# Interleaving two arrays: the first tile as two sub-tiles that are contiguous in HBM

## The chip, the cores and the metric

The kernel runs on one core of a Trainium2 chip. The metric is the time of one execution on the device in microseconds (us). For the kernel before, the median of three runs is 314.14 us (314.09 to 314.22).

The core has 16 DMA engines that move data between HBM and the on-chip memory (SBUF, 128 partitions). DMAs are issued here from two queues: SyncE's (SP, named q1 in the profile) and ScalarE's (ACT, named q10). VectorE (DVE) does the copying inside SBUF. The engines run at their own pace and wait for each other through semaphores; a DMA adds 16 to its semaphore when all of it has landed.

## The reference

The inputs x and y are float32 arrays of 32 x 256 x 1024 elements (33.6 MB each). The output has twice as many elements in its last dimension, with x in the even and y in the odd places:

```
result = np.zeros((batch, seq, dim * 2), dtype=np.float32)
result[..., 0::2] = x
result[..., 1::2] = y
```

There is no arithmetic. 67.1 MB are read and 67.1 MB are written.

## The kernel before

All three arrays are taken as flat. A tile is 128 partitions by W = 8192 elements of x and of y, 32 KiB a partition (4 MiB of each input), and gives 64 KiB a partition of output. There are n = 8 tiles, k = 0 to 7. H = W/2 = 4096 is half a tile's row. The function `rows` gives tile k of an array as 128 rows that adjoin in HBM, so a whole tile of input has rows of 32 KiB, 32 KiB apart, and a tile of output has rows of 64 KiB.

In SBUF there are two buffers each for x, y and the output (`xt`, `yt`, `ot`). Tile k uses xt and yt number k % 2. Its output is made in two halves, h = 0 and 1, and half h always goes to ot number h.

Three engines have work, each in its own order:

- SP issues the loads (lines 42 to 53). The first tile of x comes in two DMAs: columns 0 to H (line 42, semaphore xsem[0]) and columns H to W (line 43, semaphore hsem), both with rows of 16 KiB that lie 32 KiB apart in HBM. Then come y's first tile in one DMA, and x and y of tile 1, all without a wait. From tile 2 on, x waits for the third of the four copies of tile k - 2 (line 48) and y for the fourth (line 51), through the semaphore `woven`, which counts copies.
- VectorE makes four copies a tile, for each half one of x into the even places of ot (line 67) and one of y into the odd places (line 70). Before half 0 it waits for x's load (line 60) and, ahead of the copy of y, for y's load (line 69). For tile 0, half 1, it waits for hsem (line 62). From tile 1 on, it waits until the store of the preceding tile from the same buffer is complete (line 64), and for tile 1, half 0, also for qsem (line 66).
- ACT issues the stores (lines 72 to 85), each after the two copies that fill the half. A store takes 32 KiB from each partition to HBM rows that lie 64 KiB apart. The very first is cut into a quarter (8 KiB rows, line 77, semaphore qsem) and the rest (24 KiB rows, line 81, semaphore osem[0]).

At the end ACT waits for the last store from ot0 and clears the semaphores as one range of numbers (lines 87 to 90); SP waits for the last store from ot1 (line 91).

Lines 104 to 122 move the first two DMAs of SP, which wait for nothing, from the body of the program into its opening block, ahead of SP's drain. In the kernel before these are the two halves of x's first tile.

Of the kernel before, what the change touches and what calls it, by code (L numbers as in the profile page):

```python
# [3 lines left out]


def _interleave(nc, x, y, out):
    P = 128
    W = 8192
    H = W // 2  # L10

    total = 1
    for s in x.shape:
        total *= s
    n = total // (P * W)
    assert n * P * W == total

    def rows(ap, names, k):
        flat = ap.rearrange("b s d -> (b s d)")
        return flat[k * names : (k + 1) * names].rearrange("(p w) -> p w", p=P)  # L20

    fp32 = mybir.dt.float32
    xt = [nc.alloc_sbuf_tensor(f"xt{b}", [P, W], fp32).ap() for b in (0, 1)]
    yt = [nc.alloc_sbuf_tensor(f"yt{b}", [P, W], fp32).ap() for b in (0, 1)]
    ot = [nc.alloc_sbuf_tensor(f"ot{b}", [P, W], fp32).ap() for b in (0, 1)]

    xsem = [nc.alloc_semaphore(f"xsem{b}") for b in (0, 1)]
    hsem = nc.alloc_semaphore("hsem")
    qsem = nc.alloc_semaphore("qsem")
    ysem = [nc.alloc_semaphore(f"ysem{b}") for b in (0, 1)]  # L30
    woven = nc.alloc_semaphore("woven")
    osem = [nc.alloc_semaphore(f"osem{b}") for b in (0, 1)]


    cuts = [0, W // 4, W]
    parts = [slice(a, b) for a, b in zip(cuts, cuts[1:])]

    xs = [rows(x, P * W, k) for k in range(n)]
    ys = [rows(y, P * W, k) for k in range(n)]
    os_ = [rows(out, 2 * P * W, k) for k in range(n)]  # L40

    nc.sync.dma_start(out=xt[0][:, :H], in_=xs[0][:, :H]).then_inc(xsem[0], 16)
    nc.sync.dma_start(out=xt[0][:, H:], in_=xs[0][:, H:]).then_inc(hsem, 16)

    for k in range(n):
        b = k % 2
        if k >= 2:
            nc.sync.wait_ge(woven, 4 * (k - 2) + 3)
        if k:
            nc.sync.dma_start(out=xt[b], in_=xs[k]).then_inc(xsem[b], 16)  # L50
        if k >= 2:
            nc.sync.wait_ge(woven, 4 * (k - 2) + 4)
        nc.sync.dma_start(out=yt[b], in_=ys[k]).then_inc(ysem[b], 16)

    for k in range(n):
        b = k % 2
        for h in (0, 1):
            c = slice(h * H, (h + 1) * H)
            if h == 0:
                nc.vector.wait_ge(xsem[b], 16 * (k // 2 + 1))  # L60
            elif k == 0:
                nc.vector.wait_ge(hsem, 16)
            if k:
                nc.vector.wait_ge(osem[h], 16 * k)
            if (k, h) == (1, 0):
                nc.vector.wait_ge(qsem, 16)
            nc.vector.tensor_copy(out=ot[h][:, 0::2], in_=xt[b][:, c]).then_inc(woven, 1)  # L67
            if h == 0:
                nc.vector.wait_ge(ysem[b], 16 * (k // 2 + 1))
            nc.vector.tensor_copy(out=ot[h][:, 1::2], in_=yt[b][:, c]).then_inc(woven, 1)  # L70

    for k in range(n):
        for h in (0, 1):
            nc.scalar.wait_ge(woven, 4 * k + 2 * h + 2)
            if (k, h) == (0, 0):
                for c in parts[:-1]:
                    nc.scalar.dma_start(
                        out=os_[k][:, c], in_=ot[h][:, c]
                    ).then_inc(qsem, 16)
                c = parts[-1]  # L80
                nc.scalar.dma_start(out=os_[k][:, c], in_=ot[h][:, c]).then_inc(osem[h], 16)
                continue
            nc.scalar.dma_start(
                out=os_[k][:, h * W : (h + 1) * W], in_=ot[h]
            ).then_inc(osem[h], 16)

    nc.scalar.wait_ge(osem[0], 16 * n)
    used = sorted(s.num for s in [*xsem, hsem, qsem, *ysem, woven, osem[0]])
    assert used == list(range(used[0], used[-1] + 1)), used
    nc.scalar.sem_clear(range(used[0], used[-1] + 1))  # L90
    nc.sync.nop(nofuse=True).wait_op(osem[1], 16 * n, "sem-ge").then_inc(
        osem[1], -16 * n
    )


def kernel(tc, x, y, out):
    nc = tc.nc
    tc.close()
    tc.compile()

    _interleave(nc, x, y, out)

    blocks = nc.main_func.blocks
    for engine in (mybir.EngineType.SP, mybir.EngineType.SP):
        opening = blocks[0].instructions
        at, moved = next(
            (b, i)
            for b in blocks[1:]
            for i in b.instructions
            if i.engine == engine and i.opcode == "DMACopy"  # L110
        )
        assert not (moved.sync_info and moved.sync_info.on_wait)
        body = at.instructions
        body.remove(moved)
        gate = next(
            n
            for n, i in enumerate(opening)
            if i.engine == engine and i.opcode == "Drain"
        )
        opening.insert(gate, moved)  # L120
        at.instructions = body
        blocks[0].instructions = opening


# [1 line left out]
_INS = ['x', 'y']  # L126
_OUTS = [((32, 256, 2048), 'float32')]


# [23 lines left out]
```

## Time and profile before

| What | Value |
|---|---|
| median of three runs | 314.14 us (314.09 to 314.22) |
| profiled execution: span | 312.9 us (the profile gives no other time of this execution) |
| VectorE busy | 72.0 us, 32 copies of 2.29 to 2.30 us |
| VectorE idle before line 67, until a store is complete | 206.5 us, 14 waits, longest 29.0 |
| VectorE idle before line 70, until y has landed | 12.3 us, 1 wait |
| VectorE idle before line 67, until x has landed | 7.3 us, 1 wait |
| DMA, both directions | 134.22 MB, mean 429 GB/s |

The page cuts the span into 40 equal slices. A digit is the busy share of a slice in tenths, so 9 means 90% or more. The line of a DMA queue has its packets, the MB moved, and the time that its packets took as a share of 16 engines' time. A packet here is what one DMA moves for one partition's row, or one of the small ones that count up a semaphore (under 512 B). Where the share of both queues, the stretch and the number of packets are known, the mean time of one packet on its DMA engine follows: share x length of the stretch x 16 / number of packets. In a timeline a line gives start, duration, engine, line of the kernel, operation, and in brackets how long the engine had been idle and what ended that. The duration of a DMA instruction on SPq or ACTq is that of issuing it.

### The profile page before, as it was taken

To read this page: it belongs to the slowest core of one execution; us is meant where nothing else is said; L and a number is where in the kernel's file an instruction comes from. 1 tells how busy PE (TensorE), PEld (TensorE's weight loads), DVE (VectorE), ACT (ScalarE), POOL (GpSimd) and SP (SyncE) were. 2 spreads that over 40 slices of the span, in tenths; PEclk is the share of its full clock that TensorE was granted. 3 is DMA by queue.
4 is the path that set the end of the run, shared out by engine and by line. 5 is a ranking of instruction groups with operands and counts; after the bars stand their busy time and mean duration, and the time that the engine had idled before them with its cause. 6 is when DMAs were issued, how large, how long until landed. Compare 5 with 4: busy or idle time off the path is not lost.

```text
span 312.9 us, 114 instructions
## 1 busy us (share of the span) xinstructions
DVE 72.0 (23%) x32; POOL 0.2 (0%) x4
## 2 busy tenths in 40 slices
DVE  0216000501305023050220503205032050415410
POOL 0000000000000000000000000000000000000000
DMA  8999999999999999999999999999999999999998
GB/s 337 467 402 436 436 402 419 452 457 415 427 444 411 461 402 469 402 469 402 469 402 465 406 440 432 423 448 402 469 402 469 402 469 402 469 402 448 423 423 381
DMA packets 4896, 134.22 MB, mean 429 GB/s; under 512 B 544, under 2 KB 544, under 8 KB 544
## 3 DMA queue, kind: packets, MB, share of 16 engines
q1 hardware_dynamic: 2448, 67.11, 50.1%
q10 hardware_dynamic: 2448, 67.11, 49.7%
HBM read 67.11 MB, written 67.11 MB: 429 GB/s over the span
## 4 chain that ended last, share of the span: by engine, by line
DMA 82%; DVE 12%; issue 0%
DMA out_dram<-ot 76%; DMA yt<-in_y_dram 6%; DVE ot L70 6%; DVE ot L67 6%
## 5 line engine op out<-in xcount | busy, mean ns | idle before, releaser
L67 DVE COPY ot<-xt 128x4096 f32<-128x4096 f32 x16 | 36.7, 2295 | 213.8 <-DMA out_dram<-ot 206.5
L70 DVE COPY ot<-yt 128x4096 f32<-128x4096 f32 x16 | 36.6, 2288 | 12.3 <-DMA yt<-in_y_dram 12.3
L137 POOL MEMSET const-bfloat16-1.0<- 128x1 bf16 x1 | 0.1, 103 | 0.0
L137 POOL MEMSET const-uint8-127<- 128x1 uint8 x1 | 0.1, 102 | 0.0
L137 POOL MEMSET const-float32-0.0<- 128x1 f32 x1 | 0.1, 100 | 0.2 <-issue 0.2
L137 POOL MEMSET const-float32-1.0<- 128x1 f32 x1 | 0.1, 99 | 0.0
## 6 DMA issues: line engine op xcount, KB each, us to landing
out_dram<-ot ACTq DMA_DIRECT2D x15, 4096.0 KB, 34.1
yt<-in_y_dram SPq DMA_DIRECT2D x8, 4096.0 KB, 41.5
xt<-in_x_dram SPq DMA_DIRECT2D x7, 4096.0 KB, 24.3
xt<-in_x_dram SPq DMA_DIRECT2D x2, 2048.0 KB, 9.5
out_dram<-ot ACTq DMA_DIRECT2D x1, 3072.0 KB, 32.8
out_dram<-ot ACTq DMA_DIRECT2D x1, 1024.0 KB, 16.3
```

Of the source, the lines that this page charges most:

```text
L67: nc.vector.tensor_copy(out=ot[h][:, 0::2], in_=xt[b][:, c]).then_inc(woven, 1)
L70: nc.vector.tensor_copy(out=ot[h][:, 1::2], in_=yt[b][:, c]).then_inc(woven, 1)
L137: nc = _bacc.Bacc("TRN2", target_bir_lowering=False, num_devices=1)
```

## The change

The first tile of 4 MiB of each input is no longer 128 rows of 32 KiB but two sub-tiles of 2 MiB, one behind the other in HBM, each with 128 rows of 16 KiB that adjoin (`narrow(x, 1)`, `narrow(y, 1)`). The first tile of output is likewise two sub-tiles of 4 MiB with 128 adjoining rows of 32 KiB (`narrow(out, 2)`). The sub-tiles go to the same places in SBUF as the halves before. The elements that a partition holds are therefore other ones than before, for x, y and the output alike.

x's first tile comes in two DMAs as before, and y's first tile now does too. The two DMAs of x both count on xsem[0], and the two of y on ysem[0]; hsem is gone. For buffer 0 the count that VectorE waits for is 16 higher, so that for tile 0 it waits for 32 on xsem[0] ahead of its first copy, and for 32 on ysem[0] ahead of the second. The quarter and the rest of the first store, and the second store, go to the sub-tiles of the output. All other tiles are as before.

```diff
-    hsem = nc.alloc_semaphore("hsem")
...
-    nc.sync.dma_start(out=xt[0][:, :H], in_=xs[0][:, :H]).then_inc(xsem[0], 16)
-    nc.sync.dma_start(out=xt[0][:, H:], in_=xs[0][:, H:]).then_inc(hsem, 16)
+    def narrow(ap, names):
+        flat = ap.rearrange("b s d -> (b s d)")
+        cut, end = names * P * H, names * P * W
+        return [
+            flat[a:b].rearrange("(p w) -> p w", p=P) for a, b in ((0, cut), (cut, end))
+        ]
+
+    xa, xb = narrow(x, 1)
+    ya, yb = narrow(y, 1)
+    oa, ob = narrow(out, 2)
+
+    nc.sync.dma_start(out=xt[0][:, :H], in_=xa).then_inc(xsem[0], 16)
+    nc.sync.dma_start(out=xt[0][:, H:], in_=xb).then_inc(xsem[0], 16)
+    nc.sync.dma_start(out=yt[0][:, :H], in_=ya).then_inc(ysem[0], 16)
+    nc.sync.dma_start(out=yt[0][:, H:], in_=yb).then_inc(ysem[0], 16)
 
-    for k in range(n):
+    for k in range(1, n):
...
     for k in range(n):
         b = k % 2
+        landed = 16 * (k // 2 + 1) + (16 if b == 0 else 0)
         for h in (0, 1):
             c = slice(h * H, (h + 1) * H)
             if h == 0:
-                nc.vector.wait_ge(xsem[b], 16 * (k // 2 + 1))
-            elif k == 0:
-                nc.vector.wait_ge(hsem, 16)
+                nc.vector.wait_ge(xsem[b], landed)
...
             if h == 0:
-                nc.vector.wait_ge(ysem[b], 16 * (k // 2 + 1))
+                nc.vector.wait_ge(ysem[b], landed)
...
             if (k, h) == (0, 0):
-                for c in parts[:-1]:
...
-                c = parts[-1]
-                nc.scalar.dma_start(out=os_[k][:, c], in_=ot[h][:, c]).then_inc(osem[h], 16)
-                continue
...
+                Q = W // 4
+                nc.scalar.dma_start(out=oa[:, :Q], in_=ot[h][:, :Q]).then_inc(qsem, 16)
+                nc.scalar.dma_start(out=oa[:, Q:], in_=ot[h][:, Q:]).then_inc(osem[h], 16)
+            elif k == 0:
+                nc.scalar.dma_start(out=ob, in_=ot[h]).then_inc(osem[h], 16)
```

More of the change, by code (lines that the diff above doesn't have):

```diff
@@ L32, in _interleave @@
     osem = [nc.alloc_semaphore(f"osem{b}") for b in (0, 1)]
-    cuts = [0, W // 4, W]
-    parts = [slice(a, b) for a, b in zip(cuts, cuts[1:])]
     xs = [rows(x, P * W, k) for k in range(n)]
@@ L48, in _interleave @@
             nc.sync.wait_ge(woven, 4 * (k - 2) + 3)
-        if k:
-            nc.sync.dma_start(out=xt[b], in_=xs[k]).then_inc(xsem[b], 16)
+        nc.sync.dma_start(out=xt[b], in_=xs[k]).then_inc(xsem[b], 16)
         if k >= 2:
@@ L75, in _interleave @@
             if (k, h) == (0, 0):
-                for c in parts[:-1]:
-                    nc.scalar.dma_start(
-                        out=os_[k][:, c], in_=ot[h][:, c]
-                    ).then_inc(qsem, 16)
-                c = parts[-1]
-                nc.scalar.dma_start(out=os_[k][:, c], in_=ot[h][:, c]).then_inc(osem[h], 16)
-                continue
-            nc.scalar.dma_start(
-                out=os_[k][:, h * W : (h + 1) * W], in_=ot[h]
-            ).then_inc(osem[h], 16)
+                Q = W // 4
[3 more added lines that the diff above has]
+                nc.scalar.dma_start(out=ob, in_=ot[h]).then_inc(osem[h], 16)
+            else:
+                nc.scalar.dma_start(
+                    out=os_[k][:, h * W : (h + 1) * W], in_=ot[h]
+                ).then_inc(osem[h], 16)
     nc.scalar.wait_ge(osem[0], 16 * n)
-    used = sorted(s.num for s in [*xsem, hsem, qsem, *ysem, woven, osem[0]])
+    used = sorted(s.num for s in [*xsem, qsem, *ysem, woven, osem[0]])
     assert used == list(range(used[0], used[-1] + 1)), used
```

## The prediction

> **What bounds the kernel now.** I read the page's top first: whether an engine or the transfers fill the span.
>
> ```profile
> span 312.9 us, 114 instructions
> DVE 72.0 (23%) x32; POOL 0.2 (0%) x4
> DMA  8999999999999999999999999999999999999998
> ...
> q1 hardware_dynamic: 2448, 67.11, 50.1%
> q10 hardware_dynamic: 2448, 67.11, 49.7%
> ```
>
> VectorE works 23% of the span; the 16 DMA engines are full in every slice but the first and last, half by loads (q1) and half by stores (q10). The waits say the same: VectorE's 206.5 us before line 67 are waits for stores to free an output buffer. So the end is set by the sum of packet times on a DMA engine, unless a queue runs dry. Next I read packet times, from the DMA view of stretches that start and end between packets.
>
> ```profile
> DMA packets 1152, 33.55 MB, mean 434 GB/s; under 512 B 128, under 2 KB 128, under 8 KB 128
> ...
> q1 hardware_dynamic: 576, 16.78, 50.2%
> q10 hardware_dynamic: 576, 16.78, 50.2%
> ```
>
> This is 100 to 177.4 us, two tiles. Without the 128 small (semaphore) packets there are 1024 of 32 KiB. Their time is 1.004 x 77.4 x 16 = 1243 us, so 1.214 us each. The two queues have equal shares: a store whose rows lie 64 KiB apart in HBM costs what a load of adjoining rows costs.
>
> ```profile
> DMA packets 176, 2.62 MB, mean 430 GB/s; under 512 B 16, under 2 KB 16, under 8 KB 16
> ...
> q1 hardware_dynamic: 176, 2.62, 100.3%
> ```
>
> This is 4 to 10.1 us: 160 packets of 16 KiB, x's first tile. 1.003 x 6.1 x 16 / 160 = 0.612 us each, so two of them cost 0.01 us more than one of 32 KiB. Two stretches were dearer:
>
> ```profile
> DMA packets 64, 1.05 MB, mean 262 GB/s; under 512 B 0, under 2 KB 0, under 8 KB 0
> ...
> q1 hardware_dynamic: 64, 1.05, 76.6%
> ```
>
> 0 to 4 us: 64 packets took 0.766 x 4 x 16 = 49.0 us, 0.766 each, which is (0.766 - 0.612) x 4 = 0.62 us too much per engine: the first packets of the run.
>
> ```profile
> q1 hardware_dynamic: 112, 3.67, 89.7%
> q10 hardware_dynamic: 37, 0.30, 7.1%
> ```
>
> 22 to 32 us, where the first 8 KiB stores join: 112 loads took 0.897 x 160 = 143.5 us, 1.281 each, (1.281 - 1.214) x 7 = 0.47 us too much per engine. Last, the timeline shows what the first tile's arrival releases.
>
> ```profile
> 0.00 0.37 SPq L42 DMA_DIRECT2D xt<-in_x_dram  x1
> ...
> 0.42 0.42 SPq L43 DMA_DIRECT2D xt<-in_x_dram  x1
> 1.90 0.33 SPq L53 DMA_DIRECT2D yt<-in_y_dram  x1
> 2.27 0.43 SPq L50 DMA_DIRECT2D xt<-in_x_dram  x1
> 2.75 0.46 SPq L53 DMA_DIRECT2D yt<-in_y_dram  x1
> 7.33 2.30 DVE L67 COPY ot<-xt 128x4096 f32<-128x4096 f32 x1 [7.33 <-DMA xt<-in_x_dram]
> 21.91 2.29 DVE L70 COPY ot<-yt 128x4096 f32<-128x4096 f32 x1 [12.28 <-DMA yt<-in_y_dram]
> ...
> 24.24 0.38 ACTq L77 DMA_DIRECT2D out_dram<-ot  x1
> ```
>
> The first x copy starts on half of x, then VectorE sits 12.28 us until all of y is there. The second half of x, 11.8 us after its issue by line 43, lands at 0.42 + 11.8 = 12.2. y, third in the queue, lands at 21.9.
>
> **The change part by part.** There is no time of the profiled execution but its span of 312.9; the median of the runs is 314.14, 1.2 more. I take that 1.2 as unchanged and make the sum on the span.
>
> *One wait for both halves of x.* xsem[0] must now reach 32, so the first copy moves from 7.33 to about 12.2 and ends at 12.2 + 2.3 = 14.5. Behind it on VectorE is the wait for y, which ends at 21.9: 7.4 us of slack, cost 0. If y came before 14.5, up to 4.9 us would be on VectorE's path. The later copy of line 67 loses the wait on hsem, which had been over for 12 us: 0.
>
> *y in two DMAs.* The wait is for ysem[0] at 32, both halves, so the first y copy doesn't start on half of y. It stays at the time at which 8 MB have come in. Its packets become 16 per engine of 0.612 instead of 8 of 1.214: 9.79 - 9.71 = +0.08 us, on the path, as the engines are full. One more semaphore packet per engine: the two-tile stretch leaves no more for its 128 than rounding (0.1% of it, 0.08 us per engine, for 8), 0 to 0.01 each; I take 0.01. Below: were 16 KiB as cheap per byte as 32 KiB, 0. Above: at 0.766, the start's price, 16 x (0.766 - 0.607) = +2.5. I take +0.09, because the packets of 4 to 10.1 us are the same size in the same queue without a start.
>
> *SP's queue.* A sixth DMA ahead of SP's first wait. Issues took 0.33 to 0.46 us, so the loads of tile 1 are issued at about 2.7 and 3.2 instead of 2.27 and 2.75. Their first packets run only once y is in, at 21.9: 19 us of cover. Without it the cost would be 0.46. SP's next instruction waits for the third copy, at 26.4. The two DMAs hoisted ahead of the drain are still x's halves, and y's first issue stays at 1.90; ACT's and POOL's queues are passed by nothing.
>
> *Adjoining rows in HBM for x's first halves.* 16 KiB rows are read 16 KiB apart instead of 32. Packets are as many and as large as before, and the trace has no row of exactly this. The nearest are 32 KiB rows that adjoin (1.214) and 16 KiB rows 32 KiB apart (0.612), both at the full rate: 0. Below: the 0.62 of the start could vanish if the start addresses' spacing caused it, -0.62. Above: it could double, +0.62. I take 0, as first packets after nothing is in flight are most simply late for the distance to memory.
>
> *The first output as 32 KiB rows that adjoin.* The quarter's 8 KiB pieces, the 24 KiB rest and the whole second store keep number and size; only their pitch goes from 64 to 32 KiB. In the two-tile stretch pitches of 64 (stores) and 32 (loads) cost the same: 0. The 0.47 where the stores join could vanish or double: -0.47 to +0.47; I take 0, since loads are what ran slow there, and loads there are tile 1's, which the change leaves alone.
>
> *One semaphore fewer.* The clear is one range as before: 0.
>
> Sum: 0 + 0.09 + 0 + 0 + 0 = +0.09, 314.14 + 0.09 = 314.23, call it 314.2. The chain of waits moves by the same 0.1 to its end: stores after the last load run from 278 to 312.5, each buffer's refill (4.5 us of copies) hidden by the other buffer's store of 9.7.
>
> **Rivals.**
>
> *A, faster: the address spacing was the cause of the two dear stretches.* For: they lie at the start and at the first stores, just the transfers that the change moves closer together; everywhere else loads cost 1.214. Against: the steady stretch shows no dependence on pitch, and later 16 KiB packets at the old spacing cost no more than 0.612. Price: both gone, -0.62 - 0.47 + 0.09 = -1.0, 313.1; one of them alone, 313.6 to 313.8. The Trainium skill ("DMA: Bandwidth & Descriptors", Latency and other measured facts) has copies slowed by large power-of-two row pitches and advises laying tiles out contiguously. Its slow cases begin at a 512 KiB pitch, and no pitch here reaches that; the trace's equal shares at 32 and 64 KiB agree that there is nothing to win in the steady part.
>
> *B, slower: an additional DMA pays a start of its own.* The first DMA lands at 7.33, the second, of equal size, 12.2 - 7.33 = 4.9 later: the first paid 2.4 for its start. If y's second half paid that on the engines, 314.2 + 2.4 = 316.6. It decides from 0.63 us of emptiness between two queued DMAs. Against: the second half of x was queued behind the first just so and shows none. The Trainium skill (same page, Anatomy of one DMA) gives about 2.0 us fixed per DMA for DMAs that GpSimd issues. By that the time would be 314.1 + 2.0 = 316.1; the 4.9 us for 2.1 MB, 430 GB/s, disagree for DMAs queued behind another from SP.
>
> *C, slower: reads packed into a narrower part of HBM run slower.* In the first 20 us the 16 engines now read within 2 MB at a time instead of 4. Price from the only row of slowed loads, 1.281 against 1.214, 5.5% of the 19.9 us (2 to 21.9) that the first tile's loads take: +1.1, 315.3. It decides from 3.2% (0.63 of 19.9), 0.63 us per 16 KiB packet. For: no run shows 16 KiB rows adjoining, and HBM is where the change acts. Against: the pitches that are shown cost the same.
>
> *D: the change does nothing for the fill.* It is part of my forecast: neither half of x or y is consumed alone.
>
> **How the numbers follow.** About 0.2%, 0.63 us, is what a measurement of this kernel can tell from no change. Forecast 0.70 at 314.2; its own range is 313.7 (one dear stretch gone) to 314.8 (one doubled). A 0.12, faster by over 0.2%; C 0.14 and B 0.04, slower by over 0.2%. To leave out no more than 2 in 10 I take the half of A and the third of C that lie nearest: 313.4 to 315.0. Faster 0.12, same 0.70, slower 0.18.
>
> **What would show it.** Right: the first line-67 copy starts at 12.2, with a wait for y after it that ends at 21.9 to 22.1; packets of 16 KiB at 0.61 us from 12 to 22; the period of two tiles still 77.4 us; first store issue at 24.3. C is right if y lands after 22.5; B if there is a gap of over 0.6 us in DMA between y's halves; A if 0 to 4 us shows packets near 0.61, or 22 to 32 us loads near 1.214. I'm wrong altogether if a queue runs dry later: a slice of the middle below 9.

## The result and the profile after

The changed kernel takes 314.46 us (median of 19 runs, 314.34 to 316.1), the kernel before 314.21 us beside it (19 runs, 314.08 to 314.6). The medians are 0.25 us apart, 0.08%. The ratio of the two is 1.0016, with a 95% interval of 1.0009 to 1.0022; it lies higher than that of the medians because 7 of the 19 runs of the changed kernel took more than 314.7 us, which none of the kernel before did. The forecast was 314.2, in a range of 313.4 to 315.0, with no change beyond 0.2% as the likeliest: by both figures the time is there, but nearly three times as far above before as the 0.09 of the sum, and with a tail that the forecast didn't have. The interval lies above 1, so here even 0.1% can be told from no change, half of what the prediction took as the least.

The profile of the changed kernel is of the run that took 316.1 us, the longest of the 19. First the top of its page:

```profile
span 314.8 us, 115 instructions
## 1 busy us (share of the span) xinstructions
DVE 72.0 (23%) x32; POOL 0.2 (0%) x4
...
DMA  9999999999999999999999999999999999999996
...
q1 hardware_dynamic: 2592, 67.11, 49.8%
q10 hardware_dynamic: 2448, 67.11, 49.4%
```

The DMA engines are full as before up to the last slice, which has fallen from 8 to 6. q1 has 144 packets more: 128 from y's rows and 16 for the semaphore. Then its timeline of the first tile:

```profile
0.41 0.42 SPq L50 DMA_DIRECT2D xt<-in_x_dram  x1
1.89 0.33 SPq L51 DMA_DIRECT2D yt<-in_y_dram  x1
2.27 0.44 SPq L52 DMA_DIRECT2D yt<-in_y_dram  x1
2.76 0.45 SPq L58 DMA_DIRECT2D xt<-in_x_dram  x1
3.25 0.46 SPq L61 DMA_DIRECT2D yt<-in_y_dram  x1
12.49 2.29 DVE L74 COPY ot<-xt 128x4096 f32<-128x4096 f32 x1 [12.49 <-DMA xt<-in_x_dram]
22.27 2.29 DVE L77 COPY ot<-yt 128x4096 f32<-128x4096 f32 x1 [7.49 <-DMA yt<-in_y_dram]
```

Everything stands in the order forecast, the first copy after both halves of x and a wait of 7.49 us for y behind it, but 0.3 us late: x at 12.49 instead of 12.2, y at 22.27 instead of 22.0. That is past the 22.1 which the prediction named as its last right value for y, and short of rival C's 22.5. Both follow from the start: by the trace's landing events the very first DMA is complete at 7.59 us, in the kernel before at 7.31. The DMA view of 0 to 4 us, and of 14 to 18.9 us, where y is read:

```profile
DMA packets 59, 0.97 MB, mean 242 GB/s; under 512 B 0, under 2 KB 0, under 8 KB 0
...
q1 hardware_dynamic: 59, 0.97, 81.7%
```

```profile
DMA packets 144, 2.10 MB, mean 428 GB/s; under 512 B 16, under 2 KB 16, under 8 KB 16
...
q1 hardware_dynamic: 144, 2.10, 99.9%
```

The first 59 packets took 0.817 x 64 / 59 = 0.886 us each, against 0.766 for the 64 of before. y's packets of 16 KiB took 0.999 x 4.9 x 16 / 128 = 0.612, just as the prediction priced them. The last 7 us (308 to 315), first of the kernel before and then of the changed one:

```profile
DMA  0009900000990000099000000000000000000000
```

```profile
DMA  0499900049990004998000400000040000000000
```

Each digit is 0.175 us, and in so fine a view a packet's time stands in the slice in which it starts. Before, the 16 engines start their packets nearly together. After, 15 of them do so, and one is some 2 us behind: its packets are the single 4s, ahead of the groups of the others and, at the end, alone after the last group. The last store is complete when its slowest engine is. This table has the 16 landings (one an engine) of the last store, worked out from the trace's landing events, in us from the span's start; `r_after` is the changed kernel in a typical run (below):

```
             first   mean    last but one   last
before       312.59  312.70  312.80         312.82
r_after      312.57  312.70  312.82         313.05
after        312.47  312.71  312.72         314.74
```

The mean engine ends at the same time in all three. The time goes by the last.

### The profile page after: what moved, and what is told of

Read it like the earlier page. It is cut to its first block, busy times and chain, and to the rows that moved or that the text cites. A ratio compares the mean times of both kernels' runs of the same rounds, so it can differ in the third digit from the quotient of the medians.

```text
span 314.8 us, 115 instructions
## 1 busy us (share of the span) xinstructions
DVE 72.0 (23%) x32; POOL 0.2 (0%) x4
## 4 chain that ended last, share of the span: by engine, by line
DMA 82%; DVE 12%; issue 0%; SPq 0%
DMA out_dram<-ot 76%; DVE ot L77 6%; DMA yt<-in_y_dram 6%; DVE ot L74 6%; SPq L51 0%
```

## The experiments

The kernel before was measured beside each experiment (314.19 to 314.23 us in the median, no run of it over 314.62). Every kernel has 11 runs, and `y_all` 4. Some of the kernels leave elements of the first tile in other places of the output than the reference has; their expectations say which.

**The changed kernel again, `r_after`.** No edit.

> The changed kernel again, as it stands, beside its parts. Packet theory (the time is the sum of packet times: y's smaller packets, and what the first packets cost at the new addresses): most executions some 0.1 to 0.3 us over the kernel before, here 314.3 to 314.5, packets of 0 to 4 us again dearer than before's 0.766 us. Straggler theory (one DMA engine is held up late in the run, which happens to any kernel): the executions spread upward from before's time without a shift of the lowest ones, and the kernel before spreads alike.

Measured: 314.41 us (314.23 to 315.29), ratio 1.001 (1.0001 to 1.0019); 2 of 11 runs over 314.7. Its profile is of a run of 314.41, span 313.1. Packets of 0 to 4 us:

```profile
q1 hardware_dynamic: 58, 0.95, 75.4%
```

0.754 x 64 / 58 = 0.832 us each, again dearer than 0.766. Both theories have a part: there is a shift of the lowest runs by 0.15 us (0.26 in the 19 runs above), and a tail beside it. But the kernel before has no tail, so chance alone doesn't make it.

**y in two DMAs, old addresses, `y2`.**

```diff
-        nc.sync.dma_start(out=yt[b], in_=ys[k]).then_inc(ysem[b], 16)
+        if k == 0:
+            nc.sync.dma_start(out=yt[0][:, :H], in_=ys[0][:, :H]).then_inc(ysem[0], 16)
+            nc.sync.dma_start(out=yt[0][:, H:], in_=ys[0][:, H:]).then_inc(ysem[0], 16)
+        else:
+            nc.sync.dma_start(out=yt[b], in_=ys[k]).then_inc(ysem[b], 16)
...
-                nc.vector.wait_ge(ysem[b], 16 * (k // 2 + 1))
+                nc.vector.wait_ge(ysem[b], 16 * (k // 2 + 1) + (16 if b == 0 else 0))
```

> The kernel before with y's first tile in two DMAs of 16 KiB rows, 32 KiB apart in HBM, and a wait for both; no address changes. Packet theory: +0.08 to +0.1 us. A start paid for each DMA: +2.4 us. Layout theory (the new addresses are what costs): no change from before but the same +0.08.

Measured: 314.28 us (314.10 to 314.44), ratio 1.0001 (0.9992 to 1.0010). The medians are 0.09 us apart, as the packets say, though the interval can't tell that from nothing. (`y_lay` below, which has the same split, is 0.03 over the kernel before.) It does exclude a start paid for each DMA, 2.4 us (0.8%).

**The first copy waits for both halves of x, `xwait`.**

```diff
-            elif k == 0:
+            if (k, h) == (0, 0):
                 nc.vector.wait_ge(hsem, 16)
```

> The kernel before, but the first copy waits for both halves of x. Packet theory: 0, with 7.4 us of VectorE's slack left ahead of y. If the later first copy mattered at all: up to the 4.9 us by which it moves.

Measured: 314.21 us, ratio 1.0 (0.9991 to 1.0009). The slack covers the wait.

**All of y in packets of 16 KiB, `y_all`.** Each y load is two DMAs as in `y2`, for all k, with a wait for 32 (k // 2 + 1).

> The kernel before with all eight tiles of y in two DMAs of 16 KiB rows each: eight times the term that the packet theory puts on the path. Packet theory: +0.6 to +0.8 us, 314.8 to 315.0, if two 16 KiB packets cost 0.01 us more than one of 32 KiB. If smaller packets are free: 0. If they pay a start each: +19 us.

Measured: 318.47 us (318.42 to 318.66), ratio 1.0136 (1.0123 to 1.015): 4.3 us, six times what I had expected. Two waits and the DMA share of stretches near the end:

```profile
DVE ot L68 <- DMA out_dram<-ot: 121.8, 8, 21.2
DVE ot L71 <- DMA yt<-in_y_dram: 99.6, 8, 14.0
```

```profile
core 0: us, DVE busy (x) POOL busy (x), PEclk, DMA share, GB/s
280.00:290.00 10.00, 0.00 (x0) 0.00 (x0) 1.00 1.03 446
290.00:292.00 2.00, 0.00 (x0) 0.00 (x0) 1.00 0.62 262
292.00:296.60 4.60, 2.60 (x2) 0.00 (x0) 1.00 0.27 114
296.60:300.00 3.40, 3.40 (x2) 0.00 (x0) 1.00 1.08 463
```

VectorE, which in the kernel before waits for stores alone after the first tile, now waits for y too, 8 times (once of them in tile 0, as before) and for up to 14 us. From 292 to 296.6 the DMA engines are 27% busy (89% before in the same stretch): y's last tile has only just come, the stores issued before it are done, and the next waits for the copies. The same stretches of the kernel before:

```profile
280.00:290.00 10.00, 4.50 (x2) 0.00 (x0) 1.00 0.97 419
290.00:292.00 2.00, 0.00 (x0) 0.00 (x0) 1.00 1.21 524
292.00:296.60 4.60, 3.07 (x2) 0.00 (x0) 1.00 0.89 385
296.60:300.00 3.40, 1.43 (x1) 0.00 (x0) 1.00 0.94 405
```

In the middle nothing is lost but what the packets cost. This is the DMA view of 100 to 138.8 us, and two copies of y that wait for their load, five tiles apart:

```profile
DMA packets 720, 16.78 MB, mean 432 GB/s; under 512 B 80, under 2 KB 80, under 8 KB 80
...
q1 hardware_dynamic: 432, 8.39, 50.3%
q10 hardware_dynamic: 288, 8.39, 50.1%
```

```profile
100.01 2.30 DVE L71 COPY ot<-yt 128x4096 f32<-128x4096 f32 x1 [13.97 <-DMA yt<-in_y_dram]
...
294.00 2.30 DVE L71 COPY ot<-yt 128x4096 f32<-128x4096 f32 x1 [14.02 <-DMA yt<-in_y_dram]
```

A whole tile's bytes (16.78 MB) pass in 38.8 us; the copies are (294.00 - 100.01) / 5 = 38.80 us a tile apart, against 38.72 before: +0.08 a tile, the term itself. Eight times that is 0.6 us. Most of the other 3.6 us is emptiness near the end: shares times lengths of the four rows add up to 16.5 of the 20 us here and to 19.4 before, 3.0 us less; where the remaining 0.6 lies isn't shown. An engine takes packets of the two queues in turn where both have some (from 200 to 212 us of `y_all` groups of 16 loads and 16 stores, one for each engine, start by turns, but for one pair of store groups), so smaller load packets mean fewer loaded bytes per stored byte. That fits what is seen, loads that fall behind and an end that starves; that it is the whole reason is argued. So the experiment meant to enlarge one term brought in another; the term itself is borne out by the middle alone.

**x's layout alone, `x_lay`.** (`x0` is the first tile of x as two sub-tiles.)

```diff
-    nc.sync.dma_start(out=xt[0][:, :H], in_=xs[0][:, :H]).then_inc(xsem[0], 16)
-    nc.sync.dma_start(out=xt[0][:, H:], in_=xs[0][:, H:]).then_inc(hsem, 16)
+    x0 = x.rearrange("b s d -> (b s d)")[: P * W].rearrange("(s p w) -> s p w", s=2, p=P)
+    nc.sync.dma_start(out=xt[0][:, :H], in_=x0[0]).then_inc(xsem[0], 16)
+    nc.sync.dma_start(out=xt[0][:, H:], in_=x0[1]).then_inc(hsem, 16)
```

> The kernel before, but x's first tile is read as two sub-tiles with adjoining rows of 16 KiB, into the same places; y and the output stay as they were, so that in the first tile of the output x's elements stand in other places. It has the changed kernel's first 2 MB of reads alone. If the first reads' addresses make the start dearer: packets of 0 to 4 us at about 0.83 us as in the changed kernel (before 0.766), the time 314.3 to 314.5 with executions over 314.7. If they do not: 314.2, and no execution over 314.7.

Measured: 314.45 us (314.33 to 316.17), ratio 1.0018 (1.0006 to 1.0030), 4 of 11 runs over 314.7. That is the whole effect. Packets of 0 to 4 us: 0.758 x 64 / 58 = 0.836 us.

```profile
q1 hardware_dynamic: 58, 0.95, 75.8%
```

**The output's layout alone, `o_lay`.** The stores of the first tile go to `oa` and `ob` as in the change, the loads stay.

> The kernel before, but the first tile's stores go to two sub-tiles with adjoining rows of 32 KiB; x and y are read as they were, so that the first tile of the output holds the elements in other places. If the stores' addresses matter: the loads beside the first stores, 22 to 32 us, at another price than 1.281 us, with a time 0.1 to 0.5 us away from before. If the start is the cause: as before, 314.2.

Measured: 314.24 us (314.13 to 314.40), ratio 0.9999 (0.9989 to 1.0008), 0.749 x 64 / 65 = 0.737 us for the first packets. Loads from 22 to 32 us cost 0.909 x 160 / 112 = 1.299 us, no other than before's 1.281. The output's part of the change does nothing.

**y's layout alone, `y_lay`.** `y2` with its two DMAs from the sub-tiles of y.

> The kernel before with y's first tile in two DMAs from two sub-tiles with adjoining rows of 16 KiB; x and the output as they were, so that in the first tile of the output y's elements stand in other places. If only what is read at the start matters: as y's split alone, 314.2 to 314.3, no execution over 314.7. If adjoining 16 KiB rows cost wherever they are read: 314.4 to 314.5.

Measured: 314.25 us (314.15 to 314.41), ratio 1.0001 (0.9992 to 1.0010). 16 KiB rows that adjoin cost nothing of their own where they are read in the third and fourth DMA.

**The changed kernel with y in one DMA, `y_one`.**

```diff
-    nc.sync.dma_start(out=yt[0][:, :H], in_=ya).then_inc(ysem[0], 16)
-    nc.sync.dma_start(out=yt[0][:, H:], in_=yb).then_inc(ysem[0], 16)
+    y0 = y.rearrange("b s d -> (b s d)")[: P * W].rearrange("(s p w) -> p s w", s=2, p=P)
+    nc.sync.dma_start(
+        out=yt[0].rearrange("p (s w) -> p s w", s=2), in_=y0
+    ).then_inc(ysem[0], 16)
...
-                nc.vector.wait_ge(ysem[b], landed)
+                nc.vector.wait_ge(ysem[b], 16 * (k // 2 + 1))
```

> The changed kernel with y's first tile in one DMA again, from the same adjoining rows of 16 KiB. Its packets are the changed kernel's; one issue and 16 semaphore packets are gone. If addresses are the cause: the changed kernel's 314.3 to 314.5. If the second DMA of y is: 314.2 to 314.3.

Measured: 314.46 us (314.32 to 315.20), ratio 1.001 (1.0001 to 1.0019), 2 of 11 over 314.7. y's second DMA has no part in it.

**The first DMA's addresses alone, `xa_only`.**

```diff
-    nc.sync.dma_start(out=xt[0][:, :H], in_=xs[0][:, :H]).then_inc(xsem[0], 16)
+    xa = x.rearrange("b s d -> (b s d)")[: P * H].rearrange("(p w) -> p w", p=P)
+    nc.sync.dma_start(out=xt[0][:, :H], in_=xa).then_inc(xsem[0], 16)
```

> The kernel before, but the first DMA alone reads adjoining rows of 16 KiB (the first 2 MB of x); x's second half, y and the output are as they were, so that in the first tile of the output some of x's elements are others than the reference has. If it is the very first DMA's addresses: 314.4 to 314.5 and some executions over 314.7, as with both halves. If the second half's addresses count as well: between 314.2 and 314.4.

Measured: 314.48 us (314.24 to 315.55), ratio 1.0014 (1.0006 to 1.0023), 4 of 11 over 314.7. One DMA, 2 of the 134 MB, carries it all. Its first packets took 0.750 x 64 / 58 = 0.828 us:

```profile
q1 hardware_dynamic: 58, 0.95, 75.0%
```

**First rows farther apart, `wide`.** Tiles 0 and 1 are the column halves of rows twice as long, for x, y and the output; x's first 16 KiB rows lie 64 KiB apart.

```diff
-    xs = [rows(x, P * W, k) for k in range(n)]
...
+    def pair(ap, w):
+        both = rows(ap, 2 * P * w, 0)
+        return [both[:, :w], both[:, w:]]
+
+    xs = pair(x, W) + [rows(x, P * W, k) for k in range(2, n)]
...
```

> The kernel before, with tiles 0 and 1 taken as the two column halves of 128 rows that are twice as long: x's first reads are 16 KiB rows 64 KiB apart (before 32, after 16), and the output stays the reference's. Spacing theory (the farther apart the 16 engines' first reads, the cheaper the start): less than 0.766 us a packet in 0 to 4 us, 0.2 to 0.4 us less at the engines, time 313.9 to 314.2. Adjoining theory (harm comes only from rows that touch): as before, 314.2.

Measured: 314.32 us (314.16 to 314.64), ratio 1.0002 (0.9994 to 1.0011), first packets 0.762 x 64 / 64 = 0.762 us. Wider spacing wins nothing at the start; from 16 to 32 KiB the price falls, from 32 to 64 it doesn't. So a price that goes on falling with the distance is out. Three readings are left, and no run here tells them apart: rows that touch, a distance below 32 KiB, and a first DMA that stays within 2 MB. A kernel whose first rows lie a little more than 16 KiB apart would tell touching from nearness.

**x's first tile in one DMA of 32 KiB rows, `x_full`, and the same with `wide`'s rows, `x_full_wide`.**

```diff
-    nc.sync.dma_start(out=xt[0][:, :H], in_=xs[0][:, :H]).then_inc(xsem[0], 16)
-    nc.sync.dma_start(out=xt[0][:, H:], in_=xs[0][:, H:]).then_inc(hsem, 16)
+    nc.sync.dma_start(out=xt[0], in_=xs[0]).then_inc(xsem[0], 16)
...
```

(`hsem` and the wait for it are left out.)

> The kernel before with x's first tile in one DMA with rows of 32 KiB. VectorE's first copy starts at about 12.2 us and still waits for y after it. Packet theory: 16 packets of 0.612 become 8 of 1.214 per engine, -0.08 us, and the first packets, now of 32 KiB, are dearer or cheaper by some tenths; 314.0 to 314.2. Start theory (what the 16 engines' first reads cost sets the difference between the versions): a time that goes with the price of 0 to 4 us, the one place at which this kernel differs from before.

> The kernel with x's first tile in one DMA of 32 KiB rows, but with tiles 0 and 1 as column halves of doubled rows, so that the 32 KiB rows lie 64 KiB apart instead of touching; the output stays the reference's. Adjoining theory: the 314.89 of the touching rows falls to 314.2 or, with 8 packets fewer, 314.1, without executions over 314.7. If the larger first packets did the harm: 314.8 to 314.9 again.

Measured: 314.89 us (314.49 to 316.36), ratio 1.0025 (1.0015 to 1.0036), 9 of 11 over 314.7; and 314.98 us (314.30 to 315.25), ratio 1.0020 (1.0011 to 1.0029), 6 of 11 over 314.7. Fewer packets, and yet slower by more than the change. Here the adjoining theory failed: taking the rows apart healed nothing. The start is no dearer either. In `x_full`, 32 packets from 0 to 4 us took 0.767 x 64 / 32 = 1.534 us, which is 0.32 over 1.214 and 0.64 per engine, as before, and y has landed at 21.59 us in the mean of the 16 engines, ahead of the 21.71 of the kernel before (landing events, as above and in what follows). The loss comes later. The landings of one store, which at 57 us are 0.26 us apart in the kernel before, are 1.77 and 1.75 apart in these two: in `x_full` four engines, in `x_full_wide` one, are about one packet (1.21 us) behind. At the last store they are 0.92 and 0.61 apart (0.24 before), with the mean at 312.90 and 312.84 (312.70 before). So here too the last engine lies farther behind the mean, 0.63 and 0.38 against 0.12, and in `x_full` the mean is late as well. Neither comes from a dear start. These two kernels also issue y's first load in the opening block, at 0.4 us instead of 1.9, as it is now SP's second DMA; whether the larger first packets or that did it stays open.

No kernel of these beats the one before.

## Why the prediction was right or wrong

*What bounds the kernel: right, but read too simply.* The DMA engines' packets set the end. The prediction summed them as a mean over 16 engines. The mean engine ends at 312.70, 312.70 and 312.71 us in the three profiles above, so by that sum the change costs nothing at all, and the whole difference lies between the mean and the last engine: 0.12 before, 0.35 in the typical run after, 2.03 in the profiled one. In the other three profiles with the change's first rows (`x_lay`, `y_one`, `xa_only`) the mean is 312.70 to 312.76 and the last 0.28 to 1.47 behind it; in `y2`, `xwait`, `o_lay`, `y_lay` and `wide` the mean is 312.61 to 312.82 and the last 0.10 to 0.26 behind.

*One wait for both halves of x: right.* 0 forecast, `xwait` shows 0 (+0.02 in the median). The first copy and the wait for y came as told.

*y in two DMAs: right as far as the runs can tell.* Forecast +0.09; `y2` gave +0.09 in the median and `y_lay` +0.03, neither told from 0 by its interval. The packets took 0.612 us, and `y_all` shows +0.08 a tile. The rule of the Trainium skill weighed as rival B, a fixed cost of about 2.0 us for each DMA ("DMA: Bandwidth & Descriptors", Anatomy of one DMA, given for GpSimd's DMAs), isn't borne out for a DMA queued behind others from SP: the interval of `y2` ends at 1.0010, 0.3 us.

*SP's queue: right.* The loads of tile 1 were issued at 2.76 and 3.25.

*Adjoining rows for x's first halves: the step that failed.* The prediction took 0 between -0.62 and +0.62. That range held, but the 0 did not. The first packets became dearer, 0.83 to 0.89 us instead of 0.766 in the five profiles that have these rows first, and 0.74 to 0.78 in the seven of kernels with 16 KiB rows that don't touch, so in both groups without exception. The mean landing of the first DMA says the same: 7.31 to 7.38 us in the five, 7.00 to 7.12 in the seven. (0.832 - 0.612) x 58 / 16 is 0.80 us too much per engine in `r_after`, 0.62 before: +0.18 on the mean engine. Rival A had the right place, the first reads, and the wrong sign. Rival C had the right sign and the wrong extent: not the reads of the first 20 us (`y_lay` shows none), but those of the first DMA alone (`xa_only`).

*The 0.47 where stores join: right to be kept at zero for the output's rows, wrong as a term of its own.* `o_lay` leaves it at 1.299 us per load. But in the changed kernel, whose loads there are the same, it went down. The DMA view of 22 to 32 us in `r_after`:

```profile
q1 hardware_dynamic: 112, 3.67, 85.7%
```

0.857 x 160 / 112 = 1.224 us per load against 1.281: -0.40 us per engine. So the start's loss and this one aren't independent: engines that are late from the start are held up less where the stores begin. It was seen in all five profiles with the dear start (1.22 to 1.24 us) and in none of the others (1.25 to 1.34); why is not shown. In the mean of the 16 landings `r_after` is 0.31 us behind the kernel before when y's first tile is in (22.02 against 21.71), 0.06 ahead at tile 1's x (32.69 against 32.75) and even at tile 1's y (46.77 in both). That is why the mean engine comes out even, and why the forecast's time fits in part by luck: it had neither the loss nor the gain. Rival A's sign for this stretch, loads near 1.214, was met, but closer rows of the first stores are not its cause, as `o_lay` shows.

*The tail: not foreseen.* Taken together, 19 of 63 runs of the five kernels with adjoining first rows took over 314.7 us, and none of the 55 runs of `y2`, `xwait`, `o_lay`, `y_lay` and `wide`. In the profiled run the loss can be dated by the copies that wait for a store. Of the changed kernel, with its start time first:

```profile
77.08 2.29 DVE L74 COPY ot<-xt 128x4096 f32<-128x4096 f32 x1 [14.77 <-DMA out_dram<-ot]
...
116.03 2.29 DVE L74 COPY ot<-xt 128x4096 f32<-128x4096 f32 x1 [14.94 <-DMA out_dram<-ot]
...
155.77 2.29 DVE L74 COPY ot<-xt 128x4096 f32<-128x4096 f32 x1 [15.42 <-DMA out_dram<-ot]
...
233.64 2.29 DVE L74 COPY ot<-xt 128x4096 f32<-128x4096 f32 x1 [14.72 <-DMA out_dram<-ot]
...
272.36 2.29 DVE L74 COPY ot<-xt 128x4096 f32<-128x4096 f32 x1 [14.74 <-DMA out_dram<-ot]
```

Of the kernel before, the same copies:

```profile
76.83 2.29 DVE L67 COPY ot<-xt 128x4096 f32<-128x4096 f32 x1 [14.76 <-DMA out_dram<-ot]
...
115.55 2.29 DVE L67 COPY ot<-xt 128x4096 f32<-128x4096 f32 x1 [14.75 <-DMA out_dram<-ot]
```

A tile takes 38.72 us before. After, the copies shown are 0.25 us later in tile 1 (77.08) and 0.48 in tile 2 (116.03), a step of 38.95; the next step, to 155.77, is 39.74, the two to 233.64 take 77.87 together, and the last, to 272.36, is again 38.72. The trace's packets say what it is: five loads of 32 KiB, at 96, 116, 135, 177 and 197 us, took 1.40, 1.55, 1.88, 1.35 and 1.49 us instead of 1.21, 1.6 us too much together. They must be one engine's: 15 engines end the last store within 0.25 us (table above), and the last lies 0.46 us behind the mean landing at 57 us and 2.03 at the end. In between the distance hardly ever shrinks. `xa_only`, whose profile is of a run of 315.55, has the same: loads of 1.41, 1.57 and 1.42 us at 77, 97 and 116 us. After 45 us no 32 KiB packet of any other profile took over 1.30 us, but for nine of 1.33 to 1.47 in `x_full`.

What stays open: why reads of 16 KiB rows that lie 16 KiB apart are dearer as the first thing that 16 engines do and nowhere else, and why an engine's later loads at times take longer. That the first DMA's addresses bring both the dear start and the tail is shown by `xa_only` against the kernel before. That the one brings the other is not: `x_full` has a tail without a dearer start, and how far the last engine lies behind the mean at the first landing doesn't tell the two groups apart (0.21 to 0.51 us in the five profiles, 0.19 to 0.37 in the seven).

## What to carry to other kernels

Where all DMA engines are full from start to end, sum packet times for the slowest engine, not for the mean one: in the profiled run the engine that was behind at 57 us made up nothing in the 255 us that followed. Look at how far the landings of one DMA lie apart, and at the first DMA's addresses and packet size, before anything that lies under the transfers; the first copy's wait moved it by 5 us and cost nothing, and the split of y at most 0.1. And be wary of making one queue's packets smaller than the other's where both are full: in `y_all` they were served in turn, one for one, and the queue with the smaller ones fell behind.

## What the runs showed of the hardware that was not expected

- The addresses of the very first 2 MB decide 0.2 to 0.3 us of the median and whether there is a tail up to 2 us: `xa_only`, 314.48 against 314.22, with 4 of 11 runs over 314.7.
- Changing all y loads from 32 to 16 KiB packets costs 0.08 us a tile in packets, but 4.3 us in all (`y_all`): the loads fall behind, and near the end the DMA engines stand empty for 3.0 us more than before.
- One load in 32 KiB rows instead of two with 16 KiB rows, with fewer packets, makes the kernel 0.66 us slower (`x_full`, 314.89 against 314.23), with the 16 engines 1.77 us apart at 57 us and 0.92 at the end.
- A single DMA engine can fall behind the other 15 by a few slow loads: five of 1.35 to 1.88 us instead of 1.21 made 1.6 us (`after`, the run of 316.1).
